# State-space tables built beside two feed-forward layers instead of one, table instructions tied to the weights' splits, memory keys' factors and bias tables on VectorE

## The chip, the cores and the metric

One core of one Trainium2 chip runs one launch of the kernel. The metric is the device time of the launch in microseconds (us). Engines are called by the profile's names: PE is TensorE, DVE VectorE, ACT ScalarE, POOL GpSimd, and SP, SyncE, only issues DMAs. PEclk is the clock granted to PE: 1.00 is its level of 2.4 GHz, 0.50 that of 1.2 GHz.

## The reference, cut to what matters

Two blocks run on 256 tokens of width 1024 in float32: a stack of two layers, then a single block with three branches.

```
for layer in range(2):
    x = x + 0.5 * swiglu(rms_norm(x), up1[layer]) @ down1[layer]        # f1_0, f1_1
    x = x + mixed(rms_norm(x))         # even: two attentions; odd: convolution and a banded
                                       # attention with a bias table rel_table
    x = x + memory_cross_attention(rms_norm(x), rms_norm(mem), ...)     # x_0, x_1
    x = x + 0.5 * swiglu(rms_norm(x), up2[layer]) @ down2[layer]        # f2_0, f2_1
h = rms_norm_2(x)                                                       # mix2
x = x + (g1 * attn(h) + g2 * glu(gelu(s5_ssm(u))) + g3 * moba(h)) @ w_out
x = rms_norm_2(x + square(relu(h @ w_ff1)) @ w_ff2)                     # ffn2, final
```

`s5_ssm` is a linear recurrence of 32 groups with 64 complex states and 16 channels each. The kernel computes it in chunks of 8 tokens, for which it needs tables that depend on the weights alone, not on x: powers of the transition (PR, PI), V (powers times the input matrix Bb), W (powers times the output matrix C), and the convolution kernel K = V times C. So they can be made at any time ahead of mix2.

## The kernel before, in words

The work runs in 11 stages: f1_0, mix_0 (even), x_0, f2_0, f1_1, mix_1 (odd), x_1, f2_1, mix2, ffn2, final. PE does nearly all of it as float32 products of two parts: each weight tile r (128x1024, 512 KB, loaded by SP into one of 4 buffers) is split by `parts` into h, a rounded copy that ACT makes (L333), and l = r - h, which DVE makes (L334). There are 6 buffers of each. PE multiplies h with both parts of the activations and l with the first part (L376, L378).

A feed-forward stage (f1_0, f2_0, f1_1, f2_1) has 22 pieces "up" (gate and up of 11 pairs) and 11 "down", in rounds: up r1 (6 pairs), down r1, up r2, down r2. Each up piece fills two PSUM banks tagged "b", of which there are four; ACT (L725) and DVE (L726) add the halves of a bank into y and so free it. DVE then does five passes of 128x512 per pair (L762 to L773) to make hid, and in the down rounds adds the result into X (L785).

PE's instructions stand in the order in which the code is written. The other engines' order is made by a list scheduler from priorities (`hp` raises them, and chains raised instructions of an engine one behind the other). Side work is written as generators; the number that one yields (`yield self.TAB`) is the time on the planner's clock after which it goes on, and so spreads its instructions over the stage. Every engine then runs its list in order: an instruction that waits holds up all that stand behind it on its engine.

The side work that the change touches:

- `ssm_params` (POOL, small tiles of 128x32): PR, PI and the factors fr, fi. A hook of f1_1 starts it at the stage's second pair.
- `ssm_prep`, started by a hook at the second pair of f2_1: it loads bc (the matrices B1, B2, C1, C2, 1 MB, on SP's queue), negates three parts on ACT, and makes on DVE Bb (6 instructions of 128x512), four tables V and four tables W (3 instructions of 128x1024 each, all at L1641). PE multiplies V with C1 into one bank (K, 32 small matmuls of 16 columns), ACT copies it to kx, DVE adds the skip term, and SP stores it to kzD. PE transposes each V (8 x 128 columns), ACT copies the result (Vi) and stores it to vinD. W is stored to woD from POOL's queue; it has one buffer. K is read back in shifted windows (ta, on POOL's queue), copied by ACT (tl, L1732) and stored to tlD. mix2 loads these three stores.
- `head_scale`, in the attentions: sums of squares of heads, then under `hp` the rsqrt (on POOL for few columns, L435 to L440) and its product with the row factors, hf (L879). `softmax64` (L905, DVE's E,min; L909, ACT's exp) and `pt64` (L919, ACT's PT) run under `hp` too, so E,min is chained behind an hf that was written before it. The mixers' attn_b overlaps with hf of the memory keys.
- `odd`: two bias tables nb (128x1024, loaded by SP) are subtracted from a mask by POOL (L1422) at the stage's start.

V and W come from the same helper; the only difference in layout is where the products are written:

```
dv = dst.rearrange(f"p {cols} -> p g s c", g=8, s=8)    # cols: "(g s c)" for V, "(g c s)" for W
tt(dv, pw(PR), mt(M1))
```

Of the kernel before, what the change touches and what calls it, by code (L numbers as in the profile page):

```python
# [199 lines left out]
class Net:  # L200
    def __init__(self, ctx, tc, d, out):
# [3 lines left out]
        self.order = mybir.DependencyInfo(mybir.DependencyClass.NoSync, mybir.DependencyReason.DATA)  # L205
        self.last = {mybir.EngineType.Activation: None, mybir.EngineType.DVE: None}
# [659 lines left out]
    def head_factors(self, ss, v, J, nh, hd, rs):  # L866
# [7 lines left out]
        y = self.rsqrt(v, J * 2 * nh)  # L874
# [61 lines left out]
    TAB = 2000.0  # L936
# [466 lines left out]
    def odd(self, nxt):  # L1403
# [14 lines left out]
        for j in range(2):  # L1418
# [3 lines left out]
            nc.gpsimd.tensor_tensor(n, self.mbr[:, None, :].to_broadcast([128, 4, 256]), n, op=OP.subtract)  # L1422
# [145 lines left out]
    def ssm_params(self):  # L1568
# [64 lines left out]
        self.spar = PR, PI, fr, fi  # L1633

    def ssm_prep(self, pp):

        nc = self.nc
        PR, PI, fr, fi = self.spar
        bc = pp.tile([128, 4, 512], FT, name="bc")
        nc.sync.dma_start(bc, self.d["bc"].rearrange("j p c -> p j c"))  # L1640
        tt = lambda o, a, b, op=OP.mult: nc.vector.tensor_tensor(o, a, b, op=op)  # L1641
        B1, B2, C1, C2 = (bc[:, j] for j in range(4))
# [5 lines left out]
        self.woD = self.tc.dram_tile([4, 128, 1024], FT, name="woD")  # L1648
        self.tlD = self.tc.dram_tile([4, 128, 1024], FT, name="tlD")
# [3 lines left out]
        nc.sync.dma_start(self.kzD[0:112], zt)  # L1653

        def table(dst, lo, M1, M2, o, cols="(g s c)"):
            def pw(z):
                return z[:, lo:lo + 8, o * 8:o * 8 + 8].rearrange("p s g -> p g s")[:, :, :, None] \
                    .to_broadcast([128, 8, 8, 16])

            def mt(z):  # L1660
                return v3(z)[:, o * 8:o * 8 + 8, None, :].to_broadcast([128, 8, 8, 16])
            dv = dst.rearrange(f"p {cols} -> p g s c", g=8, s=8)
            t3 = pp.tile([128, 1024], FT, name="t3", tag="t3")
            tv = t3.rearrange(f"p {cols} -> p g s c", g=8, s=8)
            tt(dv, pw(PR), mt(M1))
            yield self.TAB
            tt(tv, pw(PI), mt(M2))
            yield self.TAB
            tt(dst, dst, t3, OP.add)
            yield self.TAB  # L1670

        def stream():
            yield 8000.0
            for z in (B2[0:64], C1[64:128], C2):
                nc.scalar.activation(z, z, AF.Copy, scale=-1.0)
                yield 600.0
            tb = pp.tile([128, 512], FT, name="tb")
            for B, M1, M2, op in ((Bb1, B1, B2, OP.add), (Bb2, B2, B1, OP.subtract)):
                tt(v3(B), v3(M1), frb)
                tt(v3(tb), v3(M2), fib)  # L1680
                yield self.TAB
                tt(B, B, tb, op)
                yield self.TAB
            Vs = []
            for o in range(4):
                V = pp.tile([128, 1024], FT, name=f"V{o}", tag=f"V{o}")
                yield from table(V, 0, Bb1, Bb2, o)
                Vs.append(V)
            bK = self.bank("b")
            for o in range(4):  # L1690
                for i in range(8):
                    gg = o * 8 + i
                    self.mm(bK[:, gg * 16:gg * 16 + 16], Vs[o][:, i * 128:(i + 1) * 128],
                            C1[:, gg * 16:gg * 16 + 16])
                    if i % 4 == 3:
                        yield 600.0
            kx = self.w512("kx")
            nc.scalar.activation(kx, bK, AF.Copy)
            ds = self.w512("ds")[0:16]
            nc.sync.dma_start(ds, self.d["dskip"].to_broadcast([16, 512]))  # L1700
            yield 5000.0
            dv = ds.rearrange("p (g c) -> p g c", g=32)
            nc.vector.tensor_mul(dv, dv, self.ident[0:16, None, 0:16].to_broadcast([16, 32, 16]))
            nc.vector.tensor_add(kx[0:16], kx[0:16], ds)
            yield 2000.0
            nc.sync.dma_start(self.kzD[112:240], kx)
            kz = self.kzD
            for o in range(4):
                W = pp.tile([128, 1024], FT, name="W", tag="W")
                yield from table(W, 1, C1, C2, o, "(g c s)")  # L1710
                nc.gpsimd.dma_start(self.woD[o], W)
                V = Vs[o]
                for q in range(2):
# [5 lines left out]
                    nc.scalar.activation(Vi, b, AF.Copy)  # L1719
                    nc.scalar.dma_start(self.vinD[o][:, q * 512:(q + 1) * 512], Vi)  # L1720
                    yield 600.0
            tas = []
            for o in range(4):
                ta = pp.tile([128, 1024], FT, name="ta", tag=f"V{o}")
# [4 lines left out]
            yield 20000.0  # L1729
            for o in range(4):  # L1730
                tl = pp.tile([128, 1024], FT, name="tl", tag=("W", "t3")[o % 2])
                nc.scalar.activation(tl.rearrange("p (g c i) -> p g i c", g=8, i=8),  # L1732
                                     tas[o].rearrange("p (i g c) -> p g i c", i=8, g=8), AF.Copy)
# [356 lines left out]
```

## Time and profile before

| | us |
|---|---|
| median of 3 runs (lowest, highest) | 1705.74 (1704.26, 1707.9) |
| the profiled execution, device time | 1706.53 |
| its span, first to last instruction | 1704.8 |
| PE busy | 1669.3, 98% of the span |
| DVE busy | 1216.0, 71% |
| ACT busy | 912.6, 54% |
| POOL busy | 272.0, 16% |
| mean granted clock | 0.988 |

Device time and span are two measures of one execution: 1.7 us lie outside the span. Busy shares are means over 1.7 ms; the stages differ, and the time of a stall is seen only in the stretch in which it lies.

### The profile page before, as it was taken

The page shows a single profiled execution, that of the slowest core. Times are in us where ns is not written, and L with a number is a line of the kernel's source. Part 1 is how long each engine was busy: PE and PEld are TensorE (multiplying, and loading weights), DVE is VectorE, ACT ScalarE, POOL GpSimd, SP SyncE. Part 2 cuts the span into 40 slices and gives each one's busy share as a digit, 9 for nine tenths or more (in the row PEclk, how much of TensorE's full clock was granted, in tenths as well). Part 3 has the DMA queues.
Part 4 walks back from the last instruction along what each step waited for, and adds up shares of the span by engine and source line. Part 5 has one row for each costly group of instructions (what it writes and reads, how often), then busy time and mean ns, then how long its engine had stood idle before and what let it go on. Part 6 is the DMA issues. An engine that isn't in the chain of part 4 may idle for free. (4 is left out here: it accounts for less than half of the span.)

```text
span 1704.8 us, 27043 instructions
## 1 busy us (share of the span) xinstructions
PE 1669.3 (98%) x10316; PEld 1488.6 (87%) x10316; DVE 1216.0 (71%) x1929; ACT 912.6 (54%) x1432; POOL 272.0 (16%) x624
## 2 busy tenths in 40 slices
PE   9999999999999999999999999899999999999997
PEld 7888887799988888888898999787899999998886
DVE  7968776674786888778857657987875544777865
ACT  6645566554654555555556546545654633554543
POOL 5800002102000008910100020000001570000000
PEclk9999999999999999999999999999999999999999
DMA  7766543353655556656544535458754555566652
GB/s 253 237 185 189 180 152 118 104 181 116 198 186 185 188 184 186 190 184 191 188 149 138 183 125 179 132 191 284 228 185 125 174 181 157 187 192 187 183 184 66
DMA packets 93106, 299.35 MB, mean 176 GB/s; under 512 B 14256, under 2 KB 20656, under 8 KB 92976
## 3 DMA queue, kind: packets, MB, share of 16 engines
q1 hardware_dynamic: 85376, 287.13, 53.1%
q0 software_dynamic: 1712, 5.77, 1.2%
q10 hardware_dynamic: 5888, 4.72, 0.9%
q8 instruction: 81, 1.33, 0.3%
q14 instruction: 49, 0.40, 0.1%
HBM read 288.70 MB, written 8.88 MB: 175 GB/s over the span
## 5 line engine op out<-in xcount | busy, mean ns | idle before, releaser
L334 DVE TENSOR_TENSOR l<-r,h 128x1024 fp32r<-128x1024 f32 x520 | 634.2, 1226 | 253.2 <-ACT h L333 251.7
L333 ACT ACTIVATE h<-r 128x1024 fp32r<-128x1024 f32 x520 | 547.0, 1057 | 393.2 <-PE b L376 156.7
L376 PE MATMUL b<-xx,h 128*128 128x512 f32 x1664 | 579.4, 400 | 1.7 <-ACT h L333 1.0
L378 PE MATMUL b<-xx,l 128*128 128x256 f32 x1456 | 410.6, 282 | 5.4 <-DVE l L334 5.3
L376 PEld LDWEIGHTS b<-xx,h 128*128 128x128 f32 x1664 | 302.0, 190 | 59.0 <-ACT h L333 1.3
L376 PE MATMUL b<-hid,h 128*128 128x512 f32 x960 | 338.4, 399 | 2.2 <-DVE X L785 2.2
L378 PEld LDWEIGHTS b<-xx,l 128*128 128x128 f32 x1456 | 277.0, 190 | 15.9 <-DVE l L334 6.9
L365 PE MATMUL b<-xx,h 128*128 128x256 f32 x960 | 280.5, 292 | 0.0
L366 PE MATMUL b<-xx,h 128*128 128x256 f32 x960 | 273.4, 285 | 0.0
L367 PE MATMUL b<-xx,l 128*128 128x256 f32 x960 | 273.3, 285 | 0.0
L378 PE MATMUL b<-hid,l 128*128 128x256 f32 x872 | 245.8, 282 | 0.0
L376 PEld LDWEIGHTS b<-hid,h 128*128 128x128 f32 x960 | 176.5, 189 | 41.0 <-issue 4.6
L365 PEld LDWEIGHTS b<-xx,h 128*128 128x128 f32 x960 | 186.1, 194 | 0.8
L366 PEld LDWEIGHTS b<-xx,h 128*128 128x128 f32 x960 | 186.1, 194 | 0.5
L367 PEld LDWEIGHTS b<-xx,l 128*128 128x128 f32 x960 | 185.8, 194 | 0.0
L378 PEld LDWEIGHTS b<-hid,l 128*128 128x128 f32 x872 | 164.5, 189 | 3.3
L725 ACT ACTIVATE y<-b 128x256 f32<-128x256 f32 x208 | 77.7, 381 | 120.9 <-PE b L376 120.4
L357 PE MATMUL b<-h,xx 128*128 128x512 f32 (+1 forms) x304 | 120.4, 396 | 0.6 <-ACT xx L461 0.6
L435 POOL TENSOR_TENSOR ry<-v,mhalf 128x2 f32<-128x2 f32 x12 | 8.5, 705 | 688.3 <-DVE v L494 688.3
L359 PE MATMUL b<-h,xx 128*128 128x512 f32 (+1 forms) x304 | 115.7, 381 | 0.3 <-DVE xx L462 0.3
L358 PE MATMUL b<-l,xx 128*128 128x512 f32 (+1 forms) x304 | 115.4, 380 | 0.0
L726 DVE TENSOR_TENSOR y<-b,y 128x256 f32<-128x256 f32 x208 | 85.4, 419 | 25.2 <-ACT y L725 25.0
(430 smaller groups left out, 1922.7 us busy)
## 6 DMA issues: line engine op xcount, KB each, us to landing
r<-up SPq DMA_DIRECT2D x176, 512.0 KB, 4.3
r<-down SPq DMA_DIRECT2D x88, 512.0 KB, 4.1
r<-sf SPq DMA_DIRECT2D x64, 512.0 KB, 3.7
r<-xkv SPq DMA_DIRECT2D x32, 512.0 KB, 3.8
r<-ein SPq DMA_DIRECT2D x24, 512.0 KB, 4.1
r<-sg SPq DMA_DIRECT2D x24, 512.0 KB, 4.3
r<-xq SPq DMA_DIRECT2D x16, 512.0 KB, 4.7
r<-xo SPq DMA_DIRECT2D x16, 512.0 KB, 4.7
```

The costliest lines, as they stand in the source:

```text
L333: nc.scalar.activation(h, r, AF.Copy)
L334: nc.vector.tensor_sub(l, r, h.bitcast(FT))
L357: mm(out, a[0], b[0], start=start, stop=False)
L358: mm(out, a[0], b[1], start=False, stop=False)
L359: mm(out, a[1], b[0], start=False, stop=stop)
L365: mm(out, a[0], x[:, 0], start=start, stop=False)
L366: mm(out, a[0], x[:, 1], start=False, stop=False)
L367: mm(out, a[1], x[:, 0], start=False, stop=stop)
L376: mm(b, a[0], x.rearrange("p j c -> p (j c)"), start=start, stop=stop)
L378: mm(b[:, 0:256], a[1], x[:, 0], start=False, stop=False)
L725: nc.scalar.activation(dst, b[:, 256:512], AF.Copy)
L726: nc.vector.tensor_add(dst, b[:, 0:256], dst)
```

## The change

`parts` notes the latest split on each engine, and `paced` ties an instruction behind it, so that the scheduler can't move it ahead of that split. TAB goes from 2000 to 6000. `ssm_params` moves from f1_1 to f2_0, and makes copies of PR and PI (PRs, PIs) in the layout that W wants. `ssm_prep` is split: `ssm_prep_in` (Bb, V, K, the transposes, kzD, vinD) runs beside f1_1, and `ssm_prep_out` (W, woD, ta, tl, tlD) beside f2_1. V and W get two buffers each; W is written in order. K is done per table, in a bank of its own each time. bc is loaded on POOL's queue, C1 and C2 a second time for f2_1; the negations go from ACT to POOL. hf is written where it is used (`head_fit`), not with the rsqrt. The odd mixer's nb goes from POOL to DVE, paced.

```diff
@@ parts
+        for i in nc.cur_bb.bb.instructions[-2:]:
+            self.split[i.engine] = i.name
         return h, l
+    @contextmanager
+    def paced(self):
+        cur = self.nc.cur_bb.bb
+        n = len(cur.instructions)
+        yield
+        for i in cur.instructions[n:]:
+            if i.engine in self.split:
+                self.tc.add_manual_dep(i, self.split[i.engine], self.order, reason="order")
@@ head_factors, norm_heads
-        y = self.rsqrt(v, J * 2 * nh)
+        return self.rsqrt(v, J * 2 * nh)
+    def head_fit(self, y, J, nh, rs):
...
-        f = self.head_scale(raws, nh, hd, rs)
+        y = self.head_scale(raws, nh, hd, rs)
         yield 6500.0
         with self.hp():
+            f = self.head_fit(y, len(raws), nh, rs)
@@ odd
-            nc.gpsimd.tensor_tensor(n, self.mbr[:, None, :].to_broadcast([128, 4, 256]), n, op=OP.subtract)
+            with self.paced():
+                nc.vector.tensor_tensor(n, self.mbr[:, None, :].to_broadcast([128, 4, 256]), n, op=OP.subtract)
@@ ssm_table (new; V with outer=True, W with outer=False)
+        if outer:
+            pw = [z[:, 0:8, gs].rearrange("p s g -> p g s")[:, :, :, None].to_broadcast([128, 8, 8, 16])
...
+        else:
+            pw = [z[:, gs, None, :].to_broadcast([128, 8, 16, 8]) for z in self.spar[4:]]
...
+        with self.paced():
+            tt(v(dst), pw[0], mt[0])
+        yield pace
+        with self.paced():
+            tt(v(t3), pw[1], mt[1])
+        yield pace
+        with self.paced():
+            tt(dst, dst, t3, OP.add)
+        yield pace
@@ ssm_prep_in
+        nc.gpsimd.dma_start(bc, self.d["bc"].rearrange("j p c -> p j c"))
...
+                nc.gpsimd.tensor_scalar(z, z, -1.0, 0.0, op0=OP.mult, op1=OP.add)
...
+                V = pp.tile([128, 1024], FT, name="V", tag="V", bufs=2)
+                yield from self.ssm_table(pp, V, Bb1, Bb2, o, pace, True)
...
+                b = self.bank("b")
...
+                with self.paced():
+                    nc.scalar.activation(bK[:, o * 128:(o + 1) * 128], b[:, 0:128], AF.Copy)
@@ ssm_prep_out
+        nc.gpsimd.dma_start(bc, self.d["bc"][2:4].rearrange("j p c -> p j c"))
...
+                W = pp.tile([128, 1024], FT, name="W", tag="W", bufs=2)
+                yield from self.ssm_table(pp, W, C1, C2, o, self.TAB, False)
+                nc.gpsimd.dma_start(self.woD[o], W)
+            for o in range(4):
+                tl = pp.tile([128, 1024], FT, name="tl", tag="W", bufs=2)
+                with self.paced():
+                    nc.scalar.activation(tl.rearrange("p (g c i) -> p g i c", g=8, i=8),
@@ main
-                               {2: early} if l == 0 else {1: params})
+                               {2: early} if l == 0 else {}, prep=self.ssm_prep_in if l else None)
...
+                yield from ffn(f"up2_{l}", f"down2_{l}", FF // 256, True, nxt[f"f2_{l}"],
+                               {} if l else {1: params}, prep=self.ssm_prep_out if l else None)
```

What follows are rows of DVE's list as the scheduler made it; line numbers of the changed kernel are some 13 to 17 higher (L334 is L335 there, L726 L739, L879 L895, L905 L922).

First, attn_b of the even mixer, where the memory keys' hf stands before:

```order
L334 TENSOR_TENSOR l<-r,h 128x1024
L862 TENSOR_REDUCE hss<-hsq 128x2
L873 TENSOR_SCALAR hv<-hss,rq 128x2
L879 TENSOR_SCALAR hf<-ry,rmem 128x2 x2
L905 ISA E,min<-b,mb 128x256
L905 ISA min 128x1
L905 ISA E,min<-b,mb 128x128
```

The same place with the change:

```order
L335 TENSOR_TENSOR l<-r,h 128x1024
L875 TENSOR_REDUCE hss<-hsq 128x2
L886 TENSOR_SCALAR hv<-hss,rq 128x2
L922 ISA E,min<-b,mb 128x256
L922 ISA min 128x1
L922 ISA E,min<-b,mb 128x128
L922 ISA min 128x1
```

The pair of hf instructions is gone from between hv and E,min; it stands 17 rows further on, ahead of the memory keys' products that read it.

Second, DVE in the middle of up r1 of f2_1 before (V_11429 and t_11430 are a table V and its scratch):

```order
L762 TENSOR_TENSOR y<-y,R 128x512
L334 TENSOR_TENSOR l<-r,h 128x1024
L726 TENSOR_TENSOR y<-b,y 128x256
L1641 TENSOR_TENSOR V_11429<-PR,Bb_11032 128x1024
L763 TENSOR_TENSOR y<-y,R 128x512
L1641 TENSOR_TENSOR t_11430<-PI,Bb_11033 128x1024
L765 TENSOR_TENSOR y<-y 128x512
L1641 TENSOR_TENSOR V_11429<-V_11429,t_11430 128x1024
L766 SCALAR_TENSOR_TENSOR hv<-t,y 128x512
L726 TENSOR_TENSOR y<-b,y 128x256 x2
L773 TENSOR_TENSOR hid<-hv,hid 128x2x256
L334 TENSOR_TENSOR l<-r,h 128x1024 x2
```

And up r1 of f2_1 with the change, from the stage's first y on (W is a table, t_11303 its scratch):

```order
L739 TENSOR_TENSOR y<-b,y 128x256
L507 TENSOR_SCALAR v<-b 128x2
L739 TENSOR_TENSOR y<-b,y 128x256
L1660 TENSOR_TENSOR W<-PRs,bc_11188 128x1024
L739 TENSOR_TENSOR y<-b,y 128x256 x2
L335 TENSOR_TENSOR l<-r,h 128x1024 x2
L739 TENSOR_TENSOR y<-b,y 128x256
L1660 TENSOR_TENSOR t_11303<-PIs,bc_11188 128x1024
L335 TENSOR_TENSOR l<-r,h 128x1024
L739 TENSOR_TENSOR y<-b,y 128x256
L335 TENSOR_TENSOR l<-r,h 128x1024
L775 TENSOR_TENSOR y<-y,R 128x512
```

Where three table instructions stood within five rows between two splits, there is now one between two splits, and no Bb or V in this stage.

Third, DVE in up r1 of f1_1 with the change, where before no table instruction stood:

```order
L335 TENSOR_TENSOR l<-r,h 128x1024
L1660 TENSOR_TENSOR V<-PR,Bb_6909 128x1024
L739 TENSOR_TENSOR y<-b,y 128x256
L335 TENSOR_TENSOR l<-r,h 128x1024
L776 TENSOR_TENSOR y<-y,R 128x512
L335 TENSOR_TENSOR l<-r,h 128x1024
L778 TENSOR_TENSOR y<-y 128x512
L1660 TENSOR_TENSOR t_7241<-PI,Bb_6910 128x1024
L779 SCALAR_TENSOR_TENSOR hv<-t,y 128x512
L739 TENSOR_TENSOR y<-b,y 128x256 x2
L786 TENSOR_TENSOR hid<-hv,hid 128x2x256
```

Here the tables V are now, at the same spacing.

## Rows read from the trace of the kernel before

**Rows 1.** Page, parts 1 and 5: busy time; weight split on ScalarE.
```profile
PE 1669.3 (98%) x10316; PEld 1488.6 (87%) x10316; DVE 1216.0 (71%) x1929; ACT 912.6 (54%) x1432; POOL 272.0 (16%) x624
...
L333 ACT ACTIVATE h<-r 128x1024 fp32r<-128x1024 f32 x520 | 547.0, 1057 | 393.2 <-PE b L376 156.7
```
**Rows 2.** Waits of PE, whole span: total, times, longest us.
```profile
PE b L378 <- DVE l L334: 5.3, 3, 4.3
PE b L386 <- DVE y L726: 4.1, 1, 4.1
PE b L382 <- ACT PT L919: 2.9, 1, 2.9
...
PE b L376 <- DVE X L785: 2.2, 1, 2.2
...
PE b L382 <- DVE ss L475: 1.6, 1, 1.6
...
PE b L376 <- DVE y L726: 0.8, 1, 0.8
```
**Rows 3.** Stretches: length, busy PE, PEld, DVE, ACT, POOL (count); PEclk, DMA share, GB/s.
```profile
631.00:700.00 69.00, 69.00 (x397) 60.10 (x395) 57.25 (x84) 40.29 (x63) 50.88 (x92) 1.00 0.59 182
631.00:819.00 188.00, 188.00 (x1069) 163.26 (x1068) 148.13 (x212) 101.83 (x146) 78.89 (x155) 1.00 0.59 186
1043.00:1260.00 217.00, 205.51 (x1164) 178.67 (x1163) 186.68 (x247) 117.30 (x166) 9.32 (x15) 0.96 0.64 206
1060.00:1104.00 44.00, 39.72 (x219) 34.27 (x218) 43.24 (x59) 21.28 (x35) 0.00 (x0) 0.95 0.46 141
```
**Rows 4.** Four short stretches, same columns as rows 3.
```profile
314.30:317.70 3.40, 2.90 (x10) 2.61 (x11) 1.22 (x5) 1.33 (x6) 0.00 (x0) 0.51 0.00 0
1099.40:1106.20 6.80, 5.66 (x18) 4.88 (x19) 6.37 (x7) 1.61 (x3) 0.00 (x0) 0.50 0.52 158
1147.20:1150.60 3.40, 3.40 (x11) 2.92 (x12) 1.41 (x5) 1.06 (x1) 0.09 (x1) 0.50 1.02 391
1177.90:1184.70 6.80, 4.87 (x17) 4.30 (x18) 1.99 (x3) 3.45 (x5) 0.90 (x1) 0.50 1.00 334
```
**Rows 5.** PE, 1043 to 1260 us, forms: the tables' matmuls and transposes.
```profile
L382 PE MATMUL b<-bc,V 128*128 128x16 f32 x64 | 7.7, 252 | 0.0
L386 PE MATMUL b<-ident,V 128*128 128x128 f32 x32 | 5.3, 292 | 4.1 <-DVE y L726 4.1
```
**Rows 6.** DVE's part of 1060 to 1104 us that line L1641 issued.
```profile
1060.00:1104.00 44.00, 14.65 (x13) 0.95 0.46 141
```
**Rows 7.** DVE, 1043 to 1260 us, forms: busy us, mean ns, idle before.
```profile
L1641 DVE TENSOR_TENSOR t<-PI,bc 128x1024 f32<-128x1024 f32 x4 | 9.2, 2312 | 0.0
L1641 DVE TENSOR_TENSOR W<-PR,bc 128x1024 f32<-128x1024 f32 x4 | 9.1, 2265 | 4.8 <-DMA woD<-W 4.8
...
L1641 DVE TENSOR_TENSOR V<-PR,Bb 128x1024 f32<-128x1024 f32 x4 | 4.9, 1222 | 0.0
...
L1641 DVE TENSOR_TENSOR Bb<-Bb,tb 128x512 f32<-128x512 f32 x2 | 1.4, 687 | 0.0
```
**Rows 8.** ScalarE's timeline in f2_1: start, length, instruction, idle before it.
```profile
1177.07 2.04 ACT L1732 ACTIVATE tl<-ta 128x1024 f32<-128x1024 f32 x1 [1.06 <-DMA woD<-W]
```
**Rows 9.** Timeline in attn_b, DVE and PE.
```profile
312.67 0.36 DVE L879 TENSOR_SCALAR hf<-ry,rmem 128x2 f32<-128x2 f32 x2 [2.26 <-POOL ry L440]
...
314.80 1.65 PE L382 MATMUL b<-Vb,PT 128*128 128x128 f32 x6 [2.92 <-ACT PT L919]
```
**Rows 10.** Timeline at the start of the odd mixer.
```profile
823.77 4.95 POOL L1422 TENSOR_TENSOR nb<-mbr,nb 128x1024 f32<-128x1024 f32 x2 [94.45 <-DMA nb<-rel]
823.85 2.63 DVE L462 SCALAR_TENSOR_TENSOR xx<-X,cols,xx 128x256 fp32r<-128x256 f32 x1
...
826.40 2.88 DVE L473 TENSOR_TENSOR ss<-ss,sq 128x512 f32<-128x512 f32 x1
...
829.88 0.58 PE L382 MATMUL b<-ones,ss 128*128 128x1 f32 x4 [1.56 <-DVE ss L475]
```

More of the change, by code (lines that the diff above doesn't have):

```diff
@@ L205, in __init__ @@
         self.order = mybir.DependencyInfo(mybir.DependencyClass.NoSync, mybir.DependencyReason.DATA)
+        self.split = {}
         self.last = {mybir.EngineType.Activation: None, mybir.EngineType.DVE: None}
@@ L935 @@
     ITER = 1500.0
-    TAB = 2000.0
+    TAB = 6000.0
     RW = 9000.0
@@ L1652, in ssm_prep @@
         nc.vector.memset(zt, 0.0)
[L1653 to L1670, printed above, removed]
+        nc.scalar.dma_start(self.kzD[0:112], zt)
+        pace = self.TAB
         def stream():
             yield 8000.0
-            for z in (B2[0:64], C1[64:128], C2):
-                nc.scalar.activation(z, z, AF.Copy, scale=-1.0)
+            for z in (B2[0:64], C1[64:128]):
+                nc.gpsimd.tensor_scalar(z, z, -1.0, 0.0, op0=OP.mult, op1=OP.add)
                 yield 600.0
@@ L1678, in stream @@
             for B, M1, M2, op in ((Bb1, B1, B2, OP.add), (Bb2, B2, B1, OP.subtract)):
[L1679 to L1684, printed above, removed]
-            for o in range(4):
[L1686 to L1689, printed above, removed]
@@ L1690, in stream @@
-            for o in range(4):
+                with self.paced():
+                    tt(v3(B), v3(M1), frb)
+                yield pace / 2
+                with self.paced():
+                    tt(v3(tb), v3(M2), fib)
+                yield pace / 2
+                with self.paced():
+                    tt(B, B, tb, op)
+                yield pace / 2
+            bK = None
+            for o in range(4):
+                V = pp.tile([128, 1024], FT, name="V", tag="V", bufs=2)
+                yield from self.ssm_table(pp, V, Bb1, Bb2, o, pace, True)
+                yield 2000.0
+                if bK is None:
+                    bK = pp.tile([128, 512], FT, name="kx")
+                b = self.bank("b")
@@ L1700, in stream @@
[L1700 to L1712, printed above, removed]
+                with self.paced():
+                    nc.scalar.activation(bK[:, o * 128:(o + 1) * 128], b[:, 0:128], AF.Copy)
@@ L2017, in main, with ffn @@
         pool = lambda st, n, b: st.enter_context(tc.tile_pool(name=n, bufs=b, reuse_waits="tile"))
-        def ffn(wi, wo, n, gated, to, hooks={}, bufs=HID):
+        def ffn(wi, wo, n, gated, to, hooks={}, bufs=HID, prep=None):
             with ExitStack() as st:
@@ L2022, in ffn @@
                 self.tmpp = pool(st, "tmp", 1) if {early, params} & set(hooks.values()) else None
+                if prep is not None and "mix2" in stages:
+                    self.evp = Ev()
+                    hooks = {1: lambda: prep(pool(st, "pp", 1))}
                 yield from self.ffn(wi, wo, n, gated, to, hooks)
+                if prep is not None and "mix2" in stages:
+                    yield self.evp, 0.0
         if stages[0] != "f1_0":
@@ L2040, in main @@
                     yield from self.xattn(l, nxt[f"x_{l}"])
-            if f"f2_{l}" in stages and l == 0:
-                yield from ffn("up2_0", "down2_0", FF // 256, True, nxt["f2_0"])
-        self.evp = Ev()
-        with ExitStack() as st:
-            def prep():
-                if "mix2" in stages:
-                    self.ssm_prep(st.enter_context(tc.tile_pool(name="pp", bufs=1, reuse_waits="tile")))
-                else:
-                    self.evp.t = self.now
-            if "f2_1" in stages:
-                self.hidp = pool(st, "hid", HID)
-                yield from self.ffn("up2_1", "down2_1", FF // 256, True, nxt["f2_1"], {1: prep})
-            else:
-                prep()
-            yield self.evp, 0.0
+            if f"f2_{l}" in stages:
+                yield from ffn(f"up2_{l}", f"down2_{l}", FF // 256, True, nxt[f"f2_{l}"],
+                               {} if l else {1: params}, prep=self.ssm_prep_out if l else None)
         if "mix2" in stages:
```

71 lines of the change are left out of this document (51 added, 20 removed).

## The prediction

> **What bounds the kernel now.** I read the page's busy times first: PE is busy 1669.3 of 1704.8 us and ACT's and DVE's means leave them far from it [rows 1]. So only time in which PE stands still, or runs at its lower clock, can be won. Next the list of PE's waits, where the reader is to see that a few single stalls make up most of it: 4.3 us for a DVE l, 4.1 us for a DVE y, 2.2 us for a DVE X and 0.8 us for another y [rows 2]; the timeline puts these four into f2_1, the stage with the tables, and together they are 11.4 us. Two more lie elsewhere: 2.9 us for ACT's PT (attn_b) and 1.6 us for DVE's ss (odd mixer) [rows 2].
>
> Then the stages against each other. f1_1 takes 188 us with PE busy all of it; f2_1, with the same weights' work, takes 217 [rows 3]. Behind the stalls PE runs at half clock: three stretches of f2_1 show 0.50 with 5.66, 3.40 and 4.87 us of work in them, and attn_b one with 2.90 us at 0.51 [rows 4]. Work at half clock takes twice its time, so half of it is lost: 2.8 + 1.7 + 2.4 = 7.0 us in f2_1 and 1.4 us in attn_b. f2_1's stalls and slow stretches are thus 11.4 + 7.0 = 18.4 us. The other way round, 217 - 188 = 29 us, less the tables' own PE work, 7.7 + 5.3 = 13.0 us of busy time [rows 5], leaves 16; busy times of pipelined matmuls are long, so the two agree well enough.
>
> Why it stalls there: from 1060 to 1104 us DVE is busy 43.24 of 44 us [rows 3], 14.65 us of it tables [rows 6]. In the up round of f1_1 DVE's ordinary work is 57.25 of 69 us [rows 3], or 0.83 us per us. At that rate 44 us want 36.5 + 14.7 = 51.2 us of DVE. It falls 7 us behind, the l that had been made ahead are used up, and PE stands 4.3 us. Two more stalls have other doors: DVE stands 4.8 us for the store of the one W buffer [rows 7], and ACT 1.06 us behind it, in a tl of 2.04 us, with y's ACT half queued behind [rows 8].
>
> **The change part by part.**
>
> f2_1. Bb, V, K and the transposes leave; of the tables' work on DVE only W stays. A W product costs 2.27 and 2.31 us now, a V product 1.22 [rows 7]. Both read PR or PI and a matrix in the same pattern, and only W's result is written with gaps; with the change it is written in order, but read in another pattern. So a W product costs between 1.22 and 2.31 us. I take 1.22, the price of an instruction of the same size and engine that writes in order. Ten of the twelve W instructions stand in up r1: 57.25 + 10 x 1.22 = 69.5 of 69 us, half a us behind, which any l made ahead covers. At 2.31 us for the seven products of the ten it would be 77 us, 8 behind, and the 4.3 us stall would be back: that is rival one. W has two buffers, and the third W begins after six other table steps, so the 4.8 us wait has its store done. tl takes the same buffers, with W's last stores behind it; the chance that ACT waits there again is rival two. The Bb that stood ahead of the first y go too, and with them the 0.8 us. I count the whole 18.4 us as won, and what comes instead as costs of their own.
>
> f1_1. It gets 6 Bb at 0.69 and 12 V instructions at 1.22 [rows 7], about 20 us with the small ones, on DVE's 148.13 of 188 us [rows 3]: 168 of 188. Up r1 is the tight place: Bb, zt and two tables, about 11.9 us, make 69.2 of 69 us. Nothing is left, but nothing grows either; below it is zero, above it is the stall of f2_1 again, 4.3 us and 2.8 us of clock. Nearest is the spacing: 0.17 us of tables per us against 0.33 in 1060 to 1104. I take 0.5 us. ssm_params, 50.88 us of POOL in that round [rows 3], goes to f2_0 and ends a stage ahead of its first reader.
>
> PE's table work moves from f2_1 to f1_1 and is the same in sum. New is that each table's K takes a "b" bank that ACT frees. ACT's copy stands behind an h split of 1.06 us [rows 1], so PE may wait from 0 to some 1.06 us four times, 4.2 us; three of the four places have little ahead of them, and I take half a us at each, 1.5 us.
>
> Loads. bc (1 MB) leaves SP's queue ahead of f2_1. The windows of K (2 MB) and C1, C2 are now issued before f2_1, on POOL's queue, where SP's weights start. From 0 (the DMAs idle there at times) to the size of the wait there now, 0.8 us [rows 2]; I take 0.5. The two negations on POOL, 64x512 and 128x512, have half the columns of a nb: at most 1.25 us each by nb's 2.5 [rows 10].
>
> attn_b. DVE stands 2.26 us for POOL's ry, then spends 0.36 us on hf, with E,min, ACT's exp and PT behind it; PE waits 2.92 us for PT [rows 9]. With hf behind the heads' E,min, 2.6 us of the 2.9 go, and the 1.4 us at half clock follow, since PE then stands only 0.3 us. hf comes 17 rows later, where ry has long come; its readers, the keys' products, stand behind it then as now. Gain 4.0 us.
>
> Odd mixer. POOL's two nb take 4.95 us, and two DVE instructions beside them 2.63 and 2.88 us [rows 10]; a 128x512 one costs 0.69 [rows 7]. The pair shrinks by some 4 us, more than PE's 1.56 us wait for ss. DVE pays 2 x 1.22 us for nb in return, behind ss and an l and ahead of v: v comes no later than now. The loads of nb have landed by then, since POOL's first could begin at 823.77 and its second right behind it [rows 10]. Gain 1.6 us.
>
> The Trainium skill, in SBUF — State Buffer, section "Who interferes with whom", says that a DVE instruction with two SBUF inputs and a GpSimd instruction that reads SBUF lock each other out for a whole instruction. The rows of nb agree (2.63 and 2.88 us beside 2.5 us of POOL each). By that rule POOL's negations at f2_1's start would hold DVE for their full length, which is rival three.
>
> Sum: 18.4 + 4.0 + 1.6 = 24.0 us won; 0.5 + 1.5 + 0.5 = 2.5 us paid; 21.5 us less. The span goes from 1704.8 to 1683.3 us, the device time of that execution from 1706.53 to 1685.0; it lay 0.8 us above the median of 1705.74, so the median goes to **1684.2 us**.
>
> **The rivals.**
>
> One: DVE stays overfull in a table round, because W's products stay at 2.31 us or because f1_1's 69.2 of 69 us doesn't hold. For it speaks that the sum is at the limit in both rounds; against it that the deficit is under 1 us, against 7 now. Each such stall costs 4.3 + 2.8 = 7.1 us: one gives 1691, two 1698.
>
> Two: ACT still waits in f2_1 for a buffer with a store behind it, and y's banks with it: the 4.1 us and 2.4 us of clock stay, 1690.7. Against it: two buffers, and steps three times as far apart.
>
> Three: POOL's negations hold DVE just when f2_1's first y are due, 2.5 us, and half clock for 1.7 us: 1688.4.
>
> Four, slower: f1_1 can't hold the tables. Its up round falls behind at each table as f2_1's did, 18.4 us of stalls and clock move there, and f2_1 keeps half its own, 9.2 us, by W: 1684.2 + 27.6 = 1711.8. It is decided by whether l is still made ahead when the first V stands; in f1_1 now PE never waits for an l (188.00 of 188 busy), and DVE was not late into its table time, as in f2_1, so I give it little.
>
> Five: the change moves the stalls within f2_1 and f1_1 without a net gain, about 1705.
>
> **How the numbers follow.** My forecast, 1679 to 1688 with the unknown costs at their ends (24.0 won with nothing paid gives 1681.7, and f2_1's whole excess by its clock is a us or two more; 4.2 us at the banks and 0.8 at the loads give 1686.7 and a little), has 0.62. Rival one has 0.18, two 0.06, three 0.06, four 0.05, five 0.03. Up to 1697 about 0.9 is covered; the range of 1679 to 1697 takes in one further stall and nearly two. A difference of 0.2%, 3.4 us, is about what a measurement of this kernel can tell from no change: its three runs spread by 3.6 us. Faster has 0.92, same 0.03, slower 0.05.
>
> **What would show it.** f2_1's length from its first to its last down piece some 28 us shorter and f1_1's some 14 longer, 13 of it the moved PE work; no PE wait above 1 us with an l, y or X of DVE in f2_1; W products at 1.22 us; no hf ahead of E,min and no half clock at attn_b; DVE's L462 and L473 at their usual length at the start of the odd mixer. I am wrong if PE shows waits for l in f1_1's up round, if W products stay above 2 us, or if PE waits for banks by whole microseconds at the K matmuls.

## The result, and the profile after

| | before | changed |
|---|---|---|
| median (lowest, highest), us | 1705.0 (1702.3, 1707.9), 4 runs | 1681.95 (1679.99, 1684.27), 4 runs |
| ratio to before, 95% interval | | 0.9865 (0.9844 to 0.9886) |
| the profiled execution: device time, span | 1706.53, 1704.8 | 1682.0, 1680.3 |
| mean granted clock | 0.988 | 0.994 |

The changed kernel's median is 23 us lower; 1684.2 was forecast, with 1679 to 1697 as the range.

The head of the page and PE's waits of the changed kernel (total, times, longest us):

```profile
span 1680.3 us, 27060 instructions
...
PE 1659.9 (99%) x10316; PEld 1481.8 (88%) x10316; DVE 1206.3 (72%) x1931; ACT 912.2 (54%) x1432; POOL 278.9 (17%) x630
```
```profile
PE b L399 <- DVE xE L1537: 2.6, 3, 1.2
PE b L395 <- POOL rstd L453: 2.2, 1, 2.2
PE b L395 <- POOL H L1835: 2.1, 1, 2.1
PE b L391 <- DVE l L335: 1.3, 2, 0.8
...
PE b L395 <- ACT PT L936: 0.3, 1, 0.3
```
The waits for l, y and X in f2_1 [rows 2] are gone: the 1.3 us for l that are left lie at the kernel's start, where every kernel below has two such waits of 0.9 to 1.5 us in all. PT has 0.3 us. What is at the top now, xE, rstd and H, lies in the attentions, at the end and in mix2.

The stretches, with the columns of [rows 3]: f1_1 and f2_1 from the first up piece to the last down piece, then the first 69 us of each, which lie in up r1:

```profile
626.00:824.00 198.00, 198.00 (x1163) 173.25 (x1163) 164.14 (x232) 106.05 (x157) 3.55 (x6) 1.00 0.63 194
1048.00:1235.00 187.00, 187.00 (x1064) 162.37 (x1063) 160.04 (x224) 112.08 (x153) 6.36 (x11) 1.00 0.68 214
626.00:695.00 69.00, 69.00 (x403) 60.33 (x403) 64.01 (x93) 38.84 (x62) 3.55 (x6) 1.00 0.58 182
1048.00:1117.00 69.00, 69.00 (x397) 60.15 (x396) 67.01 (x93) 42.55 (x67) 5.15 (x8) 1.00 0.65 208
```
PE is busy all of each, at the clock 1.00. DVE has 64.0 and 67.0 of 69 us in the up rounds, against 43.24 of 44 at the crowded place of before.

The other places: W's products (DVE by form, busy us and mean ns), PE's wait for PT in attn_b, and DVE at the start of the odd mixer:

```profile
L1660 DVE TENSOR_TENSOR W<-PRs,bc 128x1024 f32<-128x1024 f32 x4 | 4.9, 1217 | 0.0
L1660 DVE TENSOR_TENSOR t<-PIs,bc 128x1024 f32<-128x1024 f32 x4 | 4.9, 1216 | 0.0
```
```profile
311.01 0.94 PE L395 MATMUL b<-Vb,PT 128*128 128x128 f32 x6 [0.30 <-ACT PT L936]
```
```profile
830.56 0.42 DVE L488 TENSOR_TENSOR ss<-ss 128x256 f32<-128x256 f32 x1
831.03 1.23 DVE L335 TENSOR_TENSOR l<-r,h 128x1024 fp32r<-128x1024 f32 x1
832.17 2.36 DVE L1440 TENSOR_TENSOR nb<-mbr,nb 128x1024 f32<-128x1024 f32 x2
834.45 0.15 DVE L507 TENSOR_SCALAR v<-b 128x2 f32<-128x2 f32 x1
```
They answer to [rows 7, 9, 10]: a W product costs 1.22 us instead of 2.27 and 2.31, E,min and PT no longer stand behind hf, and nb follows ss and an l on DVE with v right behind.

For the account I take the time from one stage's row-sum product (PE's first b<-ones,ss) to the next's. It repeats to 0.1 us from kernel to kernel in a stage that is not touched (f2_0 has 187.4 us in all but one of the kernels below), while the first 20 us of a launch vary by a microsecond or two, and mix2 goes from 249.5 to 252.9 us in the kernels that have it as in the changed kernel and no long wait ahead of it. f2_1 and mix2 are read together where work crosses their border.

| us | mix_0 | f1_1 | x_1 | f2_1 | mix2 |
|---|---|---|---|---|---|
| before | 180.0 | 188.4 | 65.4 | 216.5 | 251.1 |
| changed | 176.2 | 197.3 | 66.5 | 187.2 | 251.0 |
| undo_fit_nb | 181.5 | 197.2 | 66.5 | 187.2 | 251.0 |
| strided_w | 176.2 | 197.2 | 65.4 | 190.2 | 252.6 |
| w_one_buffer | 176.2 | 197.2 | 65.4 | 187.6 | 249.5 |
| tab2000 | 176.2 | 196.9 | 65.4 | 193.0 | 252.7 |
| tie_bb | 176.2 | 197.2 | 65.4 | 187.2 | 252.9 |
| unpaced (f2_0: 231.2) | 176.3 | 197.1 | 65.4 | 189.9 | 251.8 |
| quad_v | 176.3 | 211.3 | 65.4 | 187.2 | 251.7 |
| one_layer | 176.2 | 186.7 | 65.4 | 204.5 | 267.4 |
| one_layer_early | 176.2 | 186.7 | 65.4 | 210.1 | 252.7 |
| before_dense_w | 181.3 | 186.7 | 65.6 | 212.3 | 251.1 |
| before_spread | 181.3 | 186.7 | 65.5 | 206.1 | 268.0 |
| y_later | 176.3 | 197.2 | 65.4 | 187.2 | 245.6 |

From before to changed: mix_0 -3.8, f1_1 +8.8, x_1 +1.0, f2_1 -29.3, mix2 -0.1, and -1.2 ahead of mix_0, in the part that varies: -24.5 us of span.

### The profile page after: what moved, and what is told of

Its sections match the earlier page's. It is cut to its first block, busy times and chain, and to the rows that moved or that the text cites. A ratio compares the mean times of both kernels' runs of the same rounds, so it can differ in the third digit from the quotient of the medians.

```text
span 1680.3 us, 27060 instructions
## 1 busy us (share of the span) xinstructions
PE 1659.9 (99%) x10316; PEld 1481.8 (88%) x10316; DVE 1206.3 (72%) x1931; ACT 912.2 (54%) x1432; POOL 278.9 (17%) x630
## 4 chain that ended last, share of the span: by engine, by line
PE 88%; POOL 4%; issue 4%; DVE 2%; ACT 1%; DMA 0%; SPq 0%; DVEq 0%; ACTq 0%; POOLq 0%
PE b L389 36%; PE b L391 16%; PE b L378 6%; PE b L379 6%; PE b L380 6%; PE b L395 5%; PE b L370 3%; PE b L372 3%; PE b L371 3%; PE b L388 2%; PE b L399 1%; POOL H L1835 1%; POOL m L1831 1%; DVE l L335 1%; POOL m L1832 1%
## 5 line engine op out<-in xcount | busy, mean ns | idle before, releaser
L335 DVE TENSOR_TENSOR l<-r,h 128x1024 fp32r<-128x1024 f32 x520 | 633.8, 1225 | 246.3 <-ACT h L334 244.7
L334 ACT ACTIVATE h<-r 128x1024 fp32r<-128x1024 f32 x520 | 546.8, 1057 | 380.4 <-PE b L389 176.0
L391 PEld LDWEIGHTS b<-xx,l 128*128 128x128 f32 x1456 | 275.0, 189 | 10.7 <-DVE l L335 1.9
L448 POOL TENSOR_TENSOR ry<-v,mhalf 128x2 f32<-128x2 f32 x12 | 10.3, 860 | 771.5 <-DVE v L507 771.4
L739 DVE TENSOR_TENSOR y<-b,y 128x256 f32<-128x256 f32 x208 | 84.6, 417 | 21.3 <-ACT y L738 20.7
```

What stands on the lines that cost most here:

```text
L391: mm(b[:, 0:256], a[1], x[:, 0], start=False, stop=False)
L739: nc.vector.tensor_add(dst, b[:, 0:256], dst)
```

## The experiments

**undo_fit_nb**

```diff
+        with self.hp():
+            f = self.head_fit(y, len(raws), nh, rs)
         yield 6500.0
         with self.hp():
-            f = self.head_fit(y, len(raws), nh, rs)
...
-                nc.vector.tensor_tensor(n, self.mbr[:, None, :].to_broadcast([128, 4, 256]), n, op=OP.subtract)
+            nc.gpsimd.tensor_tensor(n, self.mbr[:, None, :].to_broadcast([128, 4, 256]), n, op=OP.subtract)
```

> The changed kernel (1682.0 us in its profiled execution) with two parts undone: hf is written with the rsqrt again, ahead of the heads' E,min, and the odd mixer's nb are back on POOL. Theory (each part removed one wait of its own): PE's wait for ACT's PT in attn_b comes back with 2.9 us against 0.3 and half clock behind it, 3.8 us in mix_0 in all; DVE's ss is late again by POOL's two nb, 1.6 us. Together 1687.4 us, 5.4 us more. Rival (the mixers' gain came from elsewhere, for example from POOL's or DMA work that moved, and the two waits turn up at the next head or at the next use of ss anyway): at most 1.5 us more, with no 2.9 us wait in attn_b.

Measured: 1687.1 us median, ratio to before 0.9886 (0.9868 to 0.9905). The sum came as expected, but by luck, since the parts did not. PE's wait for PT is back (first row), and mix_0 takes 5.2 us more. The odd mixer's start costs nothing: f1_1, which reaches to it, has 197.2 us as in the changed kernel, although two DVE instructions beside POOL's nb are long again (second fence, DVE):

```profile
PE b L395 <- ACT PT L937: 2.9, 1, 2.9
```
```profile
836.99 2.51 DVE L488 TENSOR_TENSOR ss<-ss 128x256 f32<-128x256 f32 x1
839.42 4.55 DVE L335 TENSOR_TENSOR l<-r,h 128x1024 fp32r<-128x1024 f32 x2
```
Here nb began a little later among DVE's instructions. It held ss (2.51 us instead of 0.42) and the l behind it, and ss was still ready when PE came to it. before_dense_w and before_spread have nb on POOL too, and 186.7 us up to that place where before had 188.4. So hf is worth about 5 us, and the 1.6 us of nb were a matter of phase, that is, of the moment at which nb began in one execution.

**strided_w**

```diff
-            pw = [z[:, gs, None, :].to_broadcast([128, 8, 16, 8]) for z in self.spar[4:]]
+            pw = [z[:, 1:9, gs].rearrange("p s g -> p g s")[:, :, :, None].to_broadcast([128, 8, 8, 16])
...
-            v = lambda z: z.rearrange("p (g c s) -> p g c s", g=8, s=8)
+            v = lambda z: z.rearrange("p (g c s) -> p g s c", g=8, s=8)
```

> The changed kernel with W's eight products written with gaps again, from PR and PI, as in the kernel before; places and spacing stay. All expect the products at 2.3 us instead of 1.22, 8.7 us more of DVE in f2_1, of which 7.6 us lie in up r1. Theory (PE stalls only when what DVE falls behind in a round is more than the lead of the l over their use): up r1 has 2.5 us of DVE idle, so DVE falls 5 us behind, and the smallest lead in that round was 7.2 us, so no stall of PE above 0.5 us and at most 1 us more in all. Rival (my prediction's first rival: the price of W's products alone brings the 4.3 us stall and its half clock back): 7 us more, 1689.

Measured: 1686.6 us, 0.9884 (0.9865 to 0.9902); f2_1 3.0 us more, mix2 1.6 and the start of the launch 1.8, the last two in stretches that vary. PE's new wait, and DVE in the up round:

```profile
PE b L389 <- DVE X L798: 2.6, 1, 2.6
```
```profile
1049.00:1118.00 69.00, 68.77 (x394) 59.80 (x394) 68.42 (x89) 40.23 (x63) 6.36 (x8) 1.00 0.61 201
```
DVE is full (68.42 of 69 us, 67.01 in the changed kernel). No l was late: the lead (from the end of an l on DVE to PE's first use of it) fell from 7.2 to 3.9 us at the least. But the first X of the down round was late by 2.6 us: PE waits for the bank that X frees, and nothing had been made ahead for it. The theory was right on l and wrong on X; the rival's stall for l did not come.

**quad_v**

```diff
         with self.paced():
+            for _ in range(3 if outer else 0):
+                tt(v(dst), pw[0], mt[0])
             tt(v(dst), pw[0], mt[0])
...
+            for _ in range(3 if outer else 0):
+                tt(v(t3), pw[1], mt[1])
             tt(v(t3), pw[1], mt[1])
```

> The changed kernel with each of the eight products for the tables V in f1_1 computed four times over into the same place (24 instructions of 1.22 us more, 29 us; same result). Theory (lead against deficit): up r1 gets 14.6 us more on top of 63.3 busy of 69, 9 us behind, and the smallest lead there was 6.4 us, so l comes late and PE stalls 2.5 to 5 us, with half clock behind it, and again in a later round since f1_1 as a whole has 34 us of DVE idle and 29 go: 4 to 12 us more. Rival (an instruction that is tied to a place behind a split can't starve PE, whatever the amount): within 1 us of the changed kernel.

Measured: 1697.5 us, 0.995 (0.9932 to 0.9967); f1_1 14.1 us more. PE waits for l:

```profile
PE b L391 <- DVE l L335: 9.2, 5, 4.5
```
Three of these, 8.1 us, lie in f1_1. The first, 4.5 us, stands in up r1, where the lead had run down to 0.7 us. A tie to a place doesn't protect PE; what counts is the amount against the lead. The theory's size, 4 to 12 us, was too small: the median is 15.6 us above the changed kernel's.

**one_layer**

```diff
-                               {2: early} if l == 0 else {}, prep=self.ssm_prep_in if l else None)
+                               {2: early} if l == 0 else {})
...
-    TAB = 6000.0
+    TAB = 4500.0
...
             nc.scalar.dma_start(self.kzD[112:240], kx)
+            yield from self.ssm_prep_out(pp, C1, C2)
```

The windows ta share V's two buffers in this kernel and the next, so that the last two are loaded behind a tl; in the changed kernel they have four of their own.

> The changed kernel with both parts of the tables beside f2_1 again, none beside f1_1, but each instruction still tied behind a split, W in order, two buffers, and spaced by 4500 on the planner's clock instead of 6000 so that they fit. Theory (what counts is the density against the lead, not the layer): DVE's demand in f2_1's rounds is about 70.5 of 69, 33 of 34 and 58 of 56 us, some 4 us behind in all against a lead of about 10 us, so no stall above 1 us and the time within 2 us of the changed kernel's. Rival (the split over two layers is what freed f2_1): with 36 us of tables in one layer the stalls of 4.3, 2.2 and 4.1 us come back at least in half, with half clock, 7 to 18 us more.

Measured: 1706.1 us, 1.0004 (0.9992 to 1.0016): all of the change's gain is gone, and the theory with it. But neither the place nor the size, 24 us, is the rival's. PE has one long wait, at the stage's end, and ACT's timeline there shows the tl:

```profile
PE b L395 <- DVE ss L488: 15.2, 1, 15.2
```
```profile
1230.78 2.38 ACT L1780 ACTIVATE tl<-ta 128x1024 f32<-128x1024 f32 x1 [1.26 <-DMA tlD<-tl]
...
1235.17 2.24 ACT L1780 ACTIVATE tl<-ta 128x1024 f32<-128x1024 f32 x1 [0.24 <-DMA woD<-W]
...
1242.32 2.04 ACT L1780 ACTIVATE tl<-ta 128x1024 f32<-128x1024 f32 x1 [3.32 <-DMA ta<-kzD]
```
Up to then no wait of PE in f2_1 is above 1.0 us. K exists only after the fourth V, goes to DRAM and back (ta), and the four tl copies of 2.0 to 2.4 us then stand on ACT between the squares of X from which ss is made, three of them waiting for a store or a load.

ACT is not all of it: PE's own order changed too. Behind the last down piece (at 1235.2 us) the changed kernel has 10.1 us of mix2's products ahead of ss; here ss comes first (second fence, one_layer, where the last down piece is at 1236.0):

```profile
1235.40 0.28 PE L378 MATMUL b<-xx,h 128*128 128x256 f32 x1
...
1245.47 0.50 PE L395 MATMUL b<-ones,ss 128*128 128x1 f32 x4
```
```profile
1251.59 0.98 PE L395 MATMUL b<-ones,ss 128*128 128x1 f32 x4 [15.19 <-DVE ss L488]
1255.42 1.22 PE L395 MATMUL b<-ident,rstd 128*128 128x128 f32 x4 [2.85 <-POOL rstd L453]
1256.30 0.56 PE L378 MATMUL b<-xx,h 128*128 128x256 f32 x1
```
The code of mix2 goes on only when the side work has ended on the planner's clock (`yield self.evp, 0.0`), and by the order of PE that comes here behind the stage's end. So those 10 us stand in mix2's 267.4 us instead of f2_1's. DVE's ss itself was ready some 15 us after the last down piece, against some 5.5 in the changed kernel. How the loss divides between ACT's copies and the order was not measured.

**one_layer_early**

```diff
-    TAB = 4500.0
+    TAB = 4000.0
...
                 nc.gpsimd.dma_start(self.woD[o], W)
-            for o in range(4):
                 tl = pp.tile([128, 1024], FT, name="tl", tag="W", bufs=2)
...
-                yield 4500.0
+                yield 1000.0
```

> As one_layer (all tables beside f2_1, none beside f1_1), but each tl stands behind its W instead of all four at the end, and the spacing is 4000, so that the last table ends ahead of the last down round. Theory (density against lead; one_layer's loss of 15 us was ACT's four tl of 2.2 us at the stage's end, between the squares of the next stage's row sums, and not tables on DVE): that stall of 15 us goes; 36 us of tables on 198 us leave DVE short by a few us in two rounds, so small stalls, 0 to 6 us more than the changed kernel. Rival (one layer can't take them, whatever their places): 15 us or more above the changed kernel, as before the change.

Measured: 1697.1 us, 0.995 (0.9936 to 0.9964), 15 us above the changed kernel: the stall at the end is gone and mix2's products stand ahead of ss again, but 15 of one_layer's 24 us stay. PE's waits, and ACT's from 1160 to 1246 us:

```profile
PE b L391 <- DVE l L335: 5.8, 5, 2.3
...
PE b L389 <- DVE X L798: 1.9, 1, 1.9
PE b L389 <- DVE y L739: 1.6, 1, 1.6
```
```profile
ACT h L334 <- DMA r<-up: 10.9, 5, 4.2
ACT h L334 <- DMA r<-down: 10.5, 7, 3.3
...
ACT tl L1779 <- DMA ta<-kzD: 4.3, 1, 4.3
```
DVE is not full there (43.4 of 55 us from 1160 to 1215). ACT stands 4.3 us for the first ta, which was issued 8 us ahead of it; h, t and y queue behind, DVE stands 5.4 us for ACT's hid, then the loads come late, and l with them. So the theory's 0 to 6 us fell again, and the rival's 15 us came. But its reason, that no places help, is not shown by two placings: what the traces show is that in one layer ACT is what the chain from V over K, DRAM and tl runs into.

**tab2000**

```diff
-    TAB = 6000.0
+    TAB = 2000.0
```

> The changed kernel with the spacing of 2000 again; split over two layers, ties, W in order and buffers stay. Theory (density against lead): the 18 table instructions of f1_1 come in its up r1, 18.7 us on 54.8 of 69, 4.5 us behind, and the 12 of f2_1 come in some 45 us, 4.6 us behind; l had 6.4 and 7.2 us of lead at the least, X next to none, so l holds and an X or y comes late by 0 to 2.5 us in each layer: 1 to 6 us more. Rival (the tie of each instruction to its place, or the split alone, does it all): within 1 us of the changed kernel. Rival (the spacing does it all): the stalls of before in both layers, 15 us or more.

Measured: 1689.3 us, 0.9911 (0.9883 to 0.9939); f2_1 5.8 us more, f1_1 nothing. PE's waits:

```profile
PE b L391 <- DVE l L335: 3.8, 4, 2.0
...
PE b L389 <- DVE X L798: 1.3, 1, 1.3
```
An l comes 2.0 us late and an X 1.3 us, with 3.4 us at half clock between them. The theory's total, 1 to 6 us, was near for f2_1, but it had l hold and only X or y late. In f1_1 the tables fitted, with a lead of 0.7 us at the least instead of 6.4.

**unpaced**

```diff
-            if i.engine in self.split:
+            if False and i.engine in self.split:
```

> The changed kernel without the ties behind splits (spacing of 6000, split and the rest stay). The scheduler now puts Bb and two and a half V into f2_0, the first Bb some 66 us into it, where the changed kernel's DVE is at 473 us. Theory (an instruction in DVE's list that waits holds up every l behind it): that Bb waits for bc, which POOL's queue issues behind ssm_params at 539 us and which lands at about 548, so DVE stands 70 us less what l is ahead, PE loses 60 to 66 us, and half clock follows: 1742 to 1750. Rival (the ties are only fine tuning, the amount per layer decides): within 3 us of the changed kernel.

Measured: 1729.9 us, 1.0146 (1.0123 to 1.0169). DVE's first Bb:

```profile
517.97 1.15 DVE L1690 TENSOR_TENSOR Bb<-bc,sfr 128x512 f32<-128x512 f32 x1 [44.43 <-DMA bc<-bc]
```
The mechanism is the expected one, 44 us instead of 70: bc landed at 517.9, not at 548. POOL reached its copy PRs at 509.2 us, against 534.4 in the changed kernel, after the same start: it ran faster while DVE stood. f2_0 takes 43.8 us more.

**tie_bb**

```diff
-        with self.paced():
-            tt(v(dst), pw[0], mt[0])
+        tt(v(dst), pw[0], mt[0])
...
```

> The changed kernel with the ties taken from the tables' instructions alone (V and W); Bb, the copies on ACT and nb keep theirs, so that nothing can run up into f2_0. Theory (the ties' use is to keep DVE's list from an instruction whose input isn't there; the spacing does the rest): no wait for bc, no stall of PE in f1_1, where the scheduler puts seven V instructions within 24 rows of up r2 against a lead of 8 to 14 us; in f2_1 the first X comes late by 2.1 us as in the run without any tie, since a table instruction and an l stand ahead of it there: 2 to 4 us more than the changed kernel. Rival (the ties are needed at each instruction): 6 us or more. Rival (they do nothing more): within 1 us.

Measured: 1684.5 us, 0.9875 (0.9838 to 0.9912); f1_1 and f2_1 as in the changed kernel to 0.1 us, the rest in mix2 and the start. The stall of 2.1 us didn't come, so the median lies in the theory's 2 to 4 us by luck (the four runs go from 1681.9 to 1689.9). The ties on V and W do nothing that these traces show; the rest of them are worth the 48 us between unpaced and the changed kernel, of which 44 lie in f2_0, behind the Bb that waits.

**w_one_buffer**

```diff
-                W = pp.tile([128, 1024], FT, name="W", tag="W", bufs=2)
+                W = pp.tile([128, 1024], FT, name="W", tag="W")
...
-                tl = pp.tile([128, 1024], FT, name="tl", tag="W", bufs=2)
+                tl = pp.tile([128, 1024], FT, name="tl", tag="W")
```

> The changed kernel with one buffer instead of two for W and tl. A W's first product must then wait until the W before it is stored, some 7 us after its sum, against a spacing of 6 us; each tl too. Theory (lead covers short waits): DVE stands 1 to 3 us three times in up r1 of f2_1, where l has 7 us of lead, and ACT about as much at the tl: PE loses at most 1 us. Rival (the second buffer is what removed the stalls of 2.2 and 4.1 us): 4 us or more.

Measured: 1682.45 us, 0.9866 (0.985 to 0.9881), f2_1 0.3 us more. ACT's wait for the stores of tl:

```profile
ACT tl L1785 <- DMA tlD<-tl: 6.8, 2, 3.9
```
ACT stood 6.8 us and PE lost nothing of note: at this spacing the lead covers it. DVE stood for a W's store only once, for 0.9 us, not three times.

**before_dense_w**

```diff
+            if lo == 1:
+                pws = [z[:, o * 8:o * 8 + 8, None, :].to_broadcast([128, 8, 16, 8]) for z in self.sps]
+                mts = [v3(z)[:, o * 8:o * 8 + 8, :, None].to_broadcast([128, 8, 16, 8]) for z in (M1, M2)]
+                vw = lambda z: z.rearrange("p (g c s) -> p g c s", g=8, s=8)
...
```

> The kernel before with W alone changed: products written in order, from the copies PRs and PIs (the copies made by POOL in f1_1); places, spacing of 2000, the one buffer and all else stay (tb, the scratch of Bb, moves to the shared scratch pool to make room). All expect W's products at 1.22 instead of 2.27 and 2.31 us, 8.6 us less of DVE from 1104 to 1182 us. Theory (each stall of before has its own door): the stall for l of 4.3 us at 1096 comes from V and stays with its clock; that for X of 2.2 us with 1.7 us of clock goes; that for y of 4.1 us hangs on ACT, which waits for W's store, and stays or shrinks: 2 to 6 us less than before. Rival (W's price is most of it): 10 us or more less.

Measured: 1700.8 us, 0.998 (0.997 to 0.999); f2_1 4.2 us less. PE's waits:

```profile
PE b L378 <- DVE l L334: 8.1, 4, 4.1
...
PE b L386 <- DVE y L726: 1.2, 1, 1.2
```
The wait for X is gone and that for y fell from 4.1 to 1.2 us, and V's stall for l stays, as expected. A second one of 2.6 us ahead of it was not expected.

**before_spread**

```diff
-    TAB = 2000.0
+    TAB = 4500.0
```

> The kernel before with the one number of the spacing changed from 2000 to 4500; all tables beside f2_1, W with gaps, one buffer, no ties. Theory (density against lead): V now takes 0.27 us per us of the up round, so the stall for l at 1096 (4.3 us and 2.8 us of clock) goes; W's 5.8 us in 13.5 us come into rounds where DVE's own work is 0.70 to 0.77, 7 to 9 us behind, with one W buffer, so X and y come late there and the stalls of 2.2 and 4.1 us stay or grow: 0 to 8 us less than before. Rival (two layers are what counts): no gain from spacing, within 2 us of before. Rival (spacing alone does it): 15 us or more less.

Measured: 1710.1 us, 1.0023 (1.0008 to 1.0038): 4 us more than before, which neither the theory nor a rival had. PE's waits:

```profile
PE b L382 <- DVE ss L475: 11.5, 1, 11.5
...
PE b L386 <- DVE y L726: 4.2, 2, 4.0
```
The stall for l is gone by the spacing alone, that for y stays, as expected. The stall for X is gone too, although W's price stayed; that was not expected. Nor were the 11.5 us at the stage's end: as in one_layer, ss comes ahead of mix2's products in PE's order, and ACT stands 10.3 us for two ta.

**y_later**

```diff
-        yield 45000.0
+        yield 50000.0
```

> The changed kernel with one number more: in mix2 the generator that multiplies the recurrence's states H goes on after 50000 instead of 45000 on the planner's clock, which puts 48 matmuls of 128x256 ahead of the first product with H. PE waits 2.1 us there for POOL's H now, with half clock in parts of the 20 us behind it (0.71 and 0.90 granted). Theory (the wait goes since 48 matmuls are some 5.7 us of work, and half clock was the echo of the wait): 2.1 us and a part of the 6 us lost at half clock, 3 to 8 us less, 1674 to 1679. Rival (the half clock comes from the thin matmuls of 128x32 themselves): 2.1 us less and no more, or nothing.

Measured: 1676.9 us, 0.9835 (0.9818 to 0.9853), 5.1 us below the changed kernel's median; mix2 5.4 us less, and 3.9 less than in the lowest of the other kernels. 1366 to 1410 us, in the changed kernel and in this one (columns of [rows 3]):

```profile
1366.00:1410.00 44.00, 41.92 (x308) 41.81 (x308) 13.18 (x14) 11.03 (x15) 9.07 (x22) 0.84 0.53 155
```
```profile
1366.00:1410.00 44.00, 44.00 (x353) 44.00 (x352) 17.63 (x20) 13.21 (x17) 10.08 (x22) 0.92 0.57 177
```
The wait of 2.1 us is gone and the clock went from 0.84 to 0.92; half clock doesn't vanish, and what brings the rest is not shown. The theory's size held; the rival's 2.1 us and no more did not.

## Why the prediction was right, point by point

**f2_1's 18.4 us.** Right: f2_1 and f1_1 together fell by 29.3 - 8.8 = 20.5 us, of which 1.6 are the odd mixer's wait that lay in before's f1_1 stretch: 18.9 us. The four stalls are not one: single edits close some and leave others. That for l goes with the spacing (before_spread) and comes back with the amount (quad_v). That for X goes with W's price (before_dense_w) and comes back with it (strided_w), but it also goes with the spacing alone (before_spread), so it has two doors. That for y hung on ACT's tl and W's time (before_dense_w leaves 1.2 us). The 0.8 us at the first y stay in both edits of the old kernel, which leave Bb there, and go with Bb. The moved PE work was put at 13.0 us of busy time; without stalls it is 10.5, from 186.7 us in the kernels with no tables beside f1_1 to 197.2. So f1_1 grew by 10.5 and not by some 14, and with 10.5 taken from f2_1's excess of 29 the two ways to the 18.4 us agree closely.

**W's price.** Taken at 1.22, measured 1.22. The choice by the nearest instruction that writes in order held. The W wait of 4.8 us, which I gave to the second buffer, would have cost nothing at the new spacing (w_one_buffer).

**Density in the up rounds.** I put DVE at 69.2 and 69.5 of 69 us; it was 64.0 in f1_1's and 67.0 in f2_1's. In f1_1's, 10.7 us of it are Bb, zt and tables, so its ordinary work is 53.4 instead of 57.25 us; in f2_1's, 10.8 are tables and 56.2 the rest, with nine W instructions in the stretch instead of ten. Of f1_1's 3.9 us some 2.4 were put off (the stretch has one l, one y and one first pass fewer, and the lead fell from some 10 to 6.4 us); the rest is instructions that are a little shorter, such as an l of 1217 instead of 1233 ns, perhaps because POOL's parameters no longer run beside them, which is not shown. So neither round was at its limit, as the sum had it.

**What the sum didn't ask.** I laid the gain to density on DVE. one_layer and one_layer_early show that the spacings of 4500 and 4000 in one layer are not enough: K's way over DRAM to tl then ends on ACT inside the stage, and 24 and 15 us are lost, the 24 in part by PE's order. With two layers K is in DRAM before f2_1 starts, and the ta are loaded ahead of the stage. That part of the mechanism is missing from the prediction; it didn't alter the number, as the change splits the tables there. How much of one_layer_early's loss is the wait for ta itself and how much the loads behind it stays open.

**The costs of 2.5 us.** Mis-sized: banks 1.5, f1_1 0.5 and loads 0.5 were all about nothing, since PE shows no wait in either stage. So 2.5 us less were paid than forecast, 0.5 us more were won in f2_1, and the start of the launch came out 1.2 us shorter. Against that, 1.0 us more went to x_1 (below), attn_b gave 0.2 us less, and the 0.8 us between the profiled execution and the median are about nothing in the result. Together that is nearly the 2.3 us by which the median lies under the forecast.

**attn_b's 4.0 us.** Right: 3.8 against that execution. Put back it costs 5.2, since two stretches of half clock follow there instead of one, as in both edits of the old kernel (181.3 us).

**The odd mixer's 1.6 us.** Right against the profile it was read from, wrong as a price: the three other kernels with nb on POOL don't pay it.

**The rivals.** One, two and three didn't come. W at its old price didn't bring rival one's stall for l (strided_w); quad_v's 29 us more in f1_1 did. POOL's negations in f2_1 took 0.62 us each, not 1.25, and PE didn't wait there. Rival four's door, l made ahead, was the right one to watch.

## What to carry to other kernels

Stalls that look like one crowded engine can be several: find for each what is queued ahead of the late instruction, and how long its result lies ready before use (l had 7 us, X none); work that fits the first may still break the second. Side work with a chain (table, DRAM, back, copy) needed a stage boundary here, because its last copies otherwise stood on an in-order engine among the work that ends the stage; and if the next stage's code waits for the side work, its products no longer cover the stage's last wait. An instruction that a scheduler may move up needs a tie if its input comes from a slow engine or a queue behind one: here one free instruction cost 44 us.

## What the runs showed that I had not expected

A two-column instruction of POOL stretches beside DVE's splits, and by how much differs between executions of the same order. In x_1 of the changed kernel:

```profile
1004.33 2.35 DVE L335 TENSOR_TENSOR l<-r,h 128x1024 fp32r<-128x1024 f32 x2
...
1004.50 3.08 POOL L448 TENSOR_TENSOR ry<-xv,mhalf 128x2 f32<-128x2 f32 x1 [3.48 <-DVE xv L1519]
```
At the same place before, with the same two l and the same start 0.16 us into the first:

```profile
1000.55 2.35 DVE L334 TENSOR_TENSOR l<-r,h 128x1024 fp32r<-128x1024 f32 x2
...
1000.71 1.61 POOL L435 TENSOR_TENSOR ry<-xv,mhalf 128x2 f32<-128x2 f32 x1 [3.47 <-DVE xv L1501]
```
Before, it ended 0.6 us behind the first l; in the changed kernel 0.6 us behind both l and the xsq of 0.42 us that follows them. Two traces of fourteen show 3.08 us, the changed kernel's and undo_fit_nb's, and the other twelve 1.61; what decides it is not shown. So the 1.0 us of x_1 is a matter of phase and not a price of the change. Beside no l the same instruction takes 0.70 us (six of the eight in the kernel before). PE's two waits for xE behind it are 1.18 and 0.71 us; undo_fit_nb, with the same 66.5 us in x_1, shows the same pair, and the kernels with 65.4 only one of 0.7. POOL's parameters in unpaced, ahead by 25 us while DVE stood, fit this, but no run separates it. The Trainium skill, SBUF — State Buffer, section "Who interferes with whom", has the rule (a DVE instruction with two SBUF inputs and a GpSimd one that reads lock each other out); the traces agree, with POOL as the side that waits, and in the prediction I had looked for it only on DVE's side.
